# A diffusion-transformer layer on one core: twelve buffers for the modulation's weights, and another order of the MLP's buffers

## The chip, the cores and the metric

One Trainium2 chip, one of its cores. The metric is the device time of one execution in microseconds (us), as the median of several runs. The core's engines are PE (matrix multiply, with its weight loads shown as PEld), DVE, ACT and POOL (elementwise work), and SP, whose queue here issues most of the DMA transfers. Each engine takes its instructions strictly in order, and so does SP's queue.

## The reference, cut to what matters

One layer over 2048 latent tokens and 256 context tokens, 1024 channels, in float32. What the change and the prediction touch:

```python
mod = silu(c) @ w_mod + b_mod              # w_mod is 1024 x 6144
sh1, sc1, g1, sh2, sc2, g2 = split(mod, 6)
p = modulate(x, sh1, sc1) @ w_in           # layer norm, then scale and shift
y = concat(neighbourhood_attention(p), rwkv_mixer(p)) @ w_out
x = layer_norm(ALPHA * x + g1 * y)
h = squared_relu(modulate(x, sh2, sc2) @ mlp_w1)
x = layer_norm(ALPHA * x + g2 * (h @ mlp_w2))
```

`modulate` needs the first 2048 columns of `w_mod` (8 MB) before the first input projection can begin.

## The kernel before, in words

The work runs in five stages, one after the other on PE: modulation (to about 47 us), the input projection with the RWKV terms (`phase1`, to about 1003 us), attention together with the RWKV chain and the output projection (`tail`, to about 2110 us), the first MLP product (`mlp1`, to about 2771 us) and the second (`mlp2`, to the end).

**Who sets the order.** The program is traced in Python; a planner then fixes, before the run, the order of instructions on every engine and in SP's queue from its own estimate of when each is ready. Earlier lines of the program have the higher priority. Semaphore waits are added for data and for memory. On chip the order is fixed: an instruction whose wait is not over holds up all that stands behind it on its engine or queue.

**Memory.** SBUF pools are laid one behind the other from the left end of each partition, in the order in which they are opened (those with `side="right"` from the right end). When a pool is closed its bytes are free for the next one. With `reuse_waits="tile"` a tile waits for the last users of exactly those earlier tiles whose bytes it takes.

**Modulation** (lines 125 to 161). Sixteen loads of 512 KB of `w_mod` (line 146) go through SP; each feeds four PE instructions on `psd` (line 117). Their buffers are shared: eight of the loads alternate between the two `wst` buffers of pool `wp`, eight between one `th` and one `pa` buffer of pool `rk`, so four are in flight or in use at a time. While they come, PE also transposes the first six input tiles (`xturn`, line 386). When all is summed, the input is scaled and written as two parts, `xh` and `xl` (`ln1`, lines 417 to 421), tiles of 24.7 KB a partition each, which lie first in pool `k1`, at the left end. The input projection reads them (line 450) until its last matrix multiply.

**Start of `tail`.** Its left pools (`at1`: masks, queries `qz`, keys `kr`; `at2`: bias table `bu`, context keys `kc`) and its right pools (chain and accumulators) are laid over what `phase1` has left.

**`mlp1`** (line 1423) multiplies by a 7-product scheme (products 1, 5, 6, 3, 7, 2, 4, in that order) for each of 32 weight groups; a unit is one product of one group, 12 matrix multiplies. The groups 0 and 1 are begun together: units 0 to 2 are products 1, 5, 6 of group 0, units 3 to 5 the same of group 1, units 6 to 9 products 3, 7, 2, 4 of group 0, units 10 to 13 those of group 1. Each unit takes on DVE a sum or difference of weight blocks (`w1s`, lines 1448 to 1457), on ACT a rounded copy `w1h` and on DVE the rest `w1l` (line 1462), into ten `w1u` buffers of 2 KB. The weights of even groups lie in pool `xp` on the right, those of odd groups in `w1src` (`w1load`, line 1419; 1 MB each). The inputs of products 1, 5, 6 (`xh`, `xl` of each) are made ahead by `xstep`; those of products 3, 7, 2, 4 are read back from memory in four loads of 1 MB (line 1469), straight into `xl`, and then split on ACT and DVE (`xsplit`, lines 1475 and 1477). The last output tile is still being finished then: its rows `xres` are stored at line 1354, and later normalised as `xlast` (lines 1500 to 1504; POOL at line 1363, DVE at 1364, store at 1365) with rows `l1gb` loaded at line 1497.

Left to right, the pools of `mlp1` are before: `x2` (eight tiles of 8 KB: xh3, xl3, xh7, xl7, xh2, xl2, xh4, xl4), `w1src` (8 KB), `w1sum` (8 KB), `w1u` (20 KB), `h1`, `osm2`. Under them lay the output projection's pools: `yacc1` (16 KB), `woh` and `wol` (32 KB each), `l1g`, `l1b`, small ones, then the two `xres` buffers. So the last four `w1u` buffers lie on the `xres` buffers; the planner hands out `w1u` buffers 0, 9, 8, 7, 6 and so on downwards.

**`mlp2`** (line 1602) puts its results `acc` on the left end and behind them six buffers of 8 KB for its weights (`wp`, line 1625, 1 MB each), handed out 0, 5, 4, 3, 2, 1; its first input loads `al` (line 1597) come behind the weights in SP's queue. Weight buffer 0 lies on xh4, which the very last unit of `mlp1` reads.

Of the kernel before, what the change touches and what calls it, by code (L numbers as in the profile page):

```python
# [8 lines left out]
F32 = mybir.dt.float32  # L9
F32R = mybir.dt.float32r  # L10
# [5 lines left out]
D = 1024  # L16
# [5 lines left out]
W = 772  # L22
# [35 lines left out]
def f32(ap):  # L58
    return ap.bitcast(F32)


class Kern:
# [62 lines left out]
    def modulation(self, meanwhile):  # L125
        nc, a = self.nc, self.a
        t = self.sm.tile([128, 16], F32, name="silt")
        cc = self.vec[:, VOFF["c"]:VOFF["c"] + 16]
        nc.scalar.activation(t, cc, AF.Tanh, scale=0.5)
        nc.vector.tensor_scalar(t, t, 0.5, 0.5, ALU.mult, ALU.add)  # L130
        nc.vector.tensor_tensor(self.sil.rearrange("p k v -> p v k"), cc.rearrange("p (v k) -> p v k", v=2),
                                t.rearrange("p (v k) -> p v k", v=2), ALU.mult)
        acc = self.psD.tile([128, 512], F32, name="psd")
        nc.vector.memset(acc, 0.0)
        meanwhile()
        bm = self.r1.tile([128, 512], F32, tag="ei", name="bm")
        self.modbias(0, 2, bm)
        i = 0
        for k in range(8):
            for s in range(2):  # L140
                if i % 2 == 0:
                    w = self.wp.tile([128, D], F32, tag="wst", name="wmod")
                else:
                    w = self.rk.tile([128, 2, 768], F32R, tag=("th", "pa")[i // 2 % 2], name="wmod")
                    w = f32(w.rearrange("p a b -> p (a b)"))[:, :D]
                self.first = nc.sync.dma_start(w, a["w_mod"][k * 128:(k + 1) * 128, s * D:(s + 1) * D]).ins
                for j in range(2):
                    self.modacc(acc, k, s * 2 + j, w[:, j * 512:(j + 1) * 512], 2)
                i += 1
        nc.vector.tensor_tensor(bm, acc, bm, ALU.add)  # L150
        tp = self.psC.tile([128, 512], F32, name="psc")
        for b in range(4):
            nc.tensor.transpose(tp[:, b * 128:(b + 1) * 128], bm[:, b * 128:(b + 1) * 128], self.ident)

        tv = tp.rearrange("p (b j v) -> p j v b", b=4, j=4)
        for j in range(4):
            o = self.m1[:, j // 2 * 2:j // 2 * 2 + 2, j % 2 * 4:j % 2 * 4 + 4]
            if j < 2:
                nc.vector.tensor_copy(o, tv[:, j, 0:2, :])
            else:  # L160
                nc.vector.tensor_scalar(o, tv[:, j, 0:2, :], 1.0, None, ALU.add)
# [52 lines left out]
    def phase1(self):  # L214
        nc, tc, a = self.nc, self.tc, self.a
        with ExitStack() as es:
            P = lambda name, bufs, **kw: self.pool(es, name, bufs, **kw)
            k1 = P("k1", 1)
            self.xh = k1.tile([128, 8, W], F32R, name="xh")
            self.xl = k1.tile([128, 8, W], F32R, name="xl")  # L220
            self.halo = k1.tile([128, 8, 4], F32, name="halo")
            self.wp = P("wp", 2)
            self.xnp = P("xnp", 2)
            self.sm = P("sm", 4)
            self.rowp = P("rowp", 2)
            self.rk = P("rk", 1)
            self.r1 = P("r1", 1)
            self.sv = P("sv", 1)
            self.psM = P("psM", 2, space=PSUM)
            self.psB = P("psB", 3, space=PSUM)  # L230
            self.psC = P("psC", 2, space=PSUM)
            self.psD = P("psD", 1, space=PSUM)
            self.psS, self.psname = self.psB, "psb"
            ORD = (0, 2, 1)
            jobs = [(sb, b) for sb in ORD for b in self.blocks()]
            self.xs = {}
            self.wq = {}
            self.modulation(lambda: (self.wload(jobs[0], True), [self.xload(0, j) for j in range(6)], self.halo_rows(),
                                     self.xturn()))
            self.p1consts(k1)  # L240
            self.halo_cols()
            self.rq, self.sq, self.mq = [], [], []
            self.swait = 2
            self.lag = None
            for n, (sb, b) in enumerate(jobs):
                if b == jobs[0][1]:
                    self.ln1(sb)
                    nxt = ORD.index(sb) + 1
                    self.speed = (0, 1, SPEED)[nxt - 1]
                    if nxt > 1:  # L250
                        self.sq += [self.solve(*x) for x in SOLVES[nxt - 2]]
                if n == 4:
                    self.mq.append(self.modulation2())
                if b == XAT and nxt < 3:
                    self.mq.append(self.xloads(ORD[nxt]))
                if n + 1 < len(jobs):
                    self.wload(jobs[n + 1])
                for _ in self.job(sb, b):
                    self.side()
            while self.rq or self.mq or self.sq or self.lag:  # L260
                self.side()
# [1161 lines left out]
    def mlp1(self, es):  # L1423
        nc, a = self.nc, self.a
        V = nc.vector
        P = lambda name, **kw: self.pool(es, name, 1, **kw)
        x2 = P("x2")
        for pr in MORD[3:]:
            self.xu[pr] = [x2.tile([128, 4, 512], F32R, name="x%s%d" % (v, pr)) for v in "hl"]
        self.srcp, sp, up, zp = P("w1src"), P("w1sum"), P("w1u"), P("h1")  # L1430
        osm = self.pool(es, "osm2", 2)
        psP = P("psP", space=PSUM)
        self.psN = psP
# [34 lines left out]
        def xload(q, pr):  # L1468
            nc.sync.dma_start(f32(self.xu[pr][1]), self.XU[q][:, XU[pr]])
# [9 lines left out]
        def square(z):  # L1479
            V.scalar_tensor_tensor(z, z, 0.0, z, ALU.max, ALU.mult)  # L1480

        for pr in MORD[3:]:
            xload(0, pr)
        self.w1load(1)

        todo = {n + 2: [lambda pr=pr, n=n: xsplit(pr, n + 3)] for n, pr in enumerate(MORD[3:])}
        for n in range(M1LEAD):
# [2 lines left out]
        for n, (g, pr) in enumerate(seq):  # L1490
            prep(n + M1LEAD)
            q, fg = g // 16, g % 16
            if pr == 1:
# [20 lines left out]
                elif g == 20:  # L1514

                    w = self.base.tile([128, 2, 1024], F32, tag="uk", name="wp")
# [10 lines left out]
            xh, xl = self.xu[pr]  # L1527
            i = 0
# [405 lines left out]
```

## Time and profile before

| what | value |
|---|---|
| median of 3 runs | 3431.05 us (3422.89 to 3433.24) |
| profiled execution, its time | 3430.26 us |
| its span in the trace | 3428.5 us |
| mean granted PE clock | 0.963 |
| DVE, ACT busy | 76%, 44% |
| DMA, mean over the span | 164 GB/s |

The profile is one execution. A line of a timeline gives the start, the time it took, engine, line, operation, what it wrote and read, and in brackets how long the engine had been idle before it and what ended the wait. A busy PE is a pipelined one; the weight loads overlap it.

### The profile page before, as it was taken

The numbers are of one execution on the slowest core, as the hardware profiler recorded it, in microseconds if no ns is written. First come the engines' busy times: TensorE is split into PE (matmuls) and PEld (weight loads), VectorE is DVE, ScalarE is ACT, GpSimd is POOL, SyncE is SP. The second block draws the span as 40 slices with busy tenths as digits, with TensorE's granted clock in tenths as the row PEclk, the third lists the DMA queues.
The fourth block names the chain that finished last, engine by engine and source line by source line (L and its number), as shares of the span: only waits on it lengthen the run. The fifth ranks groups of instructions, "written<-read, shape, count | busy, mean of one in ns | idle before, by whom it ended". The sixth has DMA issues, their size and how long they took to land. (4 is left out here: it accounts for less than half of the span.)

```text
span 3428.5 us, 65249 instructions
## 1 busy us (share of the span) xinstructions
PE 3193.7 (93%) x25176; PEld 2605.3 (76%) x25176; DVE 2603.2 (76%) x4907; ACT 1523.1 (44%) x2891; POOL 511.6 (15%) x535
## 2 busy tenths in 40 slices
PE   7999899899978999989879988999999989999998
PEld 3888888789866777767657766777788868888886
DVE  5567977888687778767768877767767657899878
ACT  4555465456535445454442123343433343337333
POOL 0000000000005454544343322000000000010001
PEclk9999999999989999999989988999999999999999
DMA  7487376726666655554374546665644455545441
GB/s 242 134 246 209 95 178 161 223 76 168 169 191 156 140 133 129 138 131 117 98 202 147 172 155 217 213 205 186 215 155 137 154 193 162 167 153 210 148 155 73
DMA packets 765338, 561.67 MB, mean 164 GB/s; under 512 B 380412, under 2 KB 653564, under 8 KB 763620
## 3 DMA queue, kind: packets, MB, share of 16 engines
q1 hardware_dynamic: 691738, 523.14, 51.8%
q10 hardware_dynamic: 73290, 34.37, 3.5%
q8 instruction: 198, 3.24, 0.4%
q14 instruction: 112, 0.92, 0.1%
HBM read 359.70 MB, written 197.66 MB: 163 GB/s over the span
## 5 line engine op out<-in xcount | busy, mean ns | idle before, releaser
L450 PE MATMUL psm<-xh,wh 128*128 128x386 f32 (+1 forms) x1104 | 381.7, 348 | 16.5 <-ACT row L453 9.9
L450 PE MATMUL psm<-xl,wh 128*128 128x386 f32 (+1 forms) x1104 | 381.4, 346 | 2.7 <-DVE xl L421 2.6
L450 PE MATMUL psm<-xh,wl 128*128 128x386 f32 (+1 forms) x1104 | 377.0, 341 | 0.0
L450 PEld LDWEIGHTS psm<-xh,wh 128*128 128x128 f32 x1104 | 210.9, 192 | 42.7 <-ACT row L453 18.7
L450 PEld LDWEIGHTS psm<-xl,wh 128*128 128x128 f32 x1104 | 210.7, 191 | 17.8 <-issue 7.3
L450 PEld LDWEIGHTS psm<-xh,wl 128*128 128x128 f32 x1104 | 210.6, 191 | 4.9 <-issue 3.7
L1531 PE MATMUL psa<-xh,w1h 128*128 128x512 f32 x512 | 204.3, 399 | 4.0 <-DVE p L1557 3.7
L1795 POOL TENSOR_TENSOR acc<-acc,g 128x1024 f32<-128x1024 f32 x8 | 28.9, 3641 | 1186.9 <-DVE acc L1738 1186.9
L1531 PE MATMUL psa<-xl,w1h 128*128 128x512 f32 x512 | 202.7, 396 | 0.0
L1531 PE MATMUL psa<-xh,w1l 128*128 128x512 f32 x512 | 201.8, 395 | 0.0
L1679 ACT CAST ah<-al 128x1024 fp32r<-128x1024 f32 x98 | 103.0, 1051 | 216.5 <-DMA al<-HU 204.8
L760 DVE TENSOR_TENSOR stmp<-mp,xp 128x1 f32<-128x1 f32 (+30 forms) x310 | 179.2, 578 | 18.3 <-POOL xp L752 6.8
L1680 DVE TENSOR_TENSOR al<-al,ah 128x1024 fp32r<-128x1024 f32 x98 | 121.3, 1237 | 86.8 <-ACT ah L1679 86.7
L436 DVE TENSOR_TENSOR wl<-wst,wh 128x1024 fp32r<-128x1024 f32 x81 | 98.7, 1219 | 92.0 <-ACT wh L435 69.6
L1462 ACT CAST w1h<-w1s 128x512 fp32r<-128x512 f32 x96 | 59.6, 621 | 238.3 <-DVE w1s L1451 84.5
L1729 PE MATMUL psqb<-uh,ah 128*128 128x512 f32 x384 | 149.6, 392 | 9.1 <-ACT uh L1635 9.1
L1729 PE MATMUL psqa<-uh,ah 128*128 128x512 f32 x400 | 154.8, 391 | 3.2 <-ACT uh L1635 3.2
L1729 PE MATMUL psqa<-ul,ah 128*128 128x512 f32 x400 | 157.3, 393 | 0.3 <-DVE ul L1635 0.3
L1729 PE MATMUL psqa<-uh,al 128*128 128x512 f32 x400 | 157.0, 392 | 0.0
L761 DVE TENSOR_REDUCE xp<-stmp 128x1 f32<-128x1 f32 (+30 forms) x310 | 153.9, 496 | 3.3
L1729 PE MATMUL psqb<-ul,ah 128*128 128x512 f32 x384 | 150.5, 392 | 0.0
L1729 PE MATMUL psqb<-uh,al 128*128 128x512 f32 x384 | 150.3, 391 | 0.0
(393 smaller groups left out, 8818.4 us busy)
## 6 DMA issues: line engine op xcount, KB each, us to landing
al<-HU SPq DMA_DIRECT2D x106, 512.0 KB, 3.6
wst<-in_w_in SPq DMA_DIRECT2D x81, 512.0 KB, 4.3
w<-in_mlp_w SPq DMA_DIRECT2D x32, 1024.0 KB, 7.7
wp<-in_mlp_w SPq DMA_DIRECT2D x32, 1024.0 KB, 6.4
wmod<-in_w_mod SPq DMA_DIRECT2D x48, 512.0 KB, 5.3
HU<-p SPq DMA_DIRECT2D x96, 256.0 KB, 3.9
HU<-s SPq DMA_DIRECT2D x84, 256.0 KB, 2.0
bkc<-BK SPq DMA_DIRECT2D x36, 512.0 KB, 4.8
```

What stands on the lines that cost most here:

```text
L436: nc.vector.tensor_tensor(wl, w, f32(wh), ALU.subtract)
L450: nc.tensor.matmul(ps[:, :y - x], lhsT=s[:, k, :], rhs=m[:, k, x:y], start=(i == 0), stop=(i == 23))
L760: nc.vector.tensor_tensor(tv, mp[:, i:i + 1, lo:lo + n].to_broadcast([128, n, n]), xp[:, lo:lo + n, lo:lo + n], ALU.mult)
L761: nc.vector.tensor_reduce(xp[:, lo:lo + n, i], tv, AX.X, ALU.add)
L1462: made[n] = nc.scalar.copy(h, x).ins, V.tensor_tensor(l, x, f32(h), ALU.subtract).ins
L1531: nc.tensor.matmul(ps, lhsT=w[:, k, :], rhs=x[:, k, :], start=(i == 0 and pr in (1, 5, 2)), stop=(i == 11), skip_group_check=True)
L1679: fs += [lambda: nc.scalar.copy(ah, f32(al)), fb[0], lambda: V.tensor_tensor(al, f32(al), f32(ah), ALU.subtract), fb[1]]
L1680: lambda: V.tensor_tensor(al, f32(al), f32(ah), ALU.subtract), fb[1]]
L1729: nc.tensor.matmul(ps, lhsT=x[:, c, s], rhs=y[:, c, :], start=(i == 0 and new), stop=(i == 5 and end), skip_group_check=True)
L1795: (V if 4 * i + j in VMUL else G).tensor_tensor(row, row, g2, ALU.mult)
```

## The change

In `modulation` the sixteen loads get buffers of their own, twelve tiles of 4 KB in a new pool `modp`. That pool is opened last in `phase1`, closed after the modulation, and a pool `kx` with `xh` and `xl` is opened in its place; they no longer lie first in `k1`, and all other pools of `phase1` move 49,408 bytes to the left. In `mlp1` the pools are opened as `w1u`, `w1src`, `w1sum`, `x2`, `h1`, and the load of the second weight group stands ahead of the four input loads in the program.

```diff
-                if i % 2 == 0:
-                    w = self.wp.tile([128, D], F32, tag="wst", name="wmod")
-                else:
-                    w = self.rk.tile([128, 2, 768], F32R, tag=("th", "pa")[i // 2 % 2], name="wmod")
-                    w = f32(w.rearrange("p a b -> p (a b)"))[:, :D]
+                w = self.modp.tile([128, D], F32, name="wmod")
                 self.first = nc.sync.dma_start(w, a["w_mod"][k * 128:(k + 1) * 128, s * D:(s + 1) * D]).ins
...
             k1 = P("k1", 1)
-            self.xh = k1.tile([128, 8, W], F32R, name="xh")
-            self.xl = k1.tile([128, 8, W], F32R, name="xl")
             self.halo = k1.tile([128, 8, 4], F32, name="halo")
...
-            self.modulation(lambda: (self.wload(jobs[0], True), [self.xload(0, j) for j in range(6)], self.halo_rows(),
-                                     self.xturn()))
+
+            with ExitStack() as em:
+                self.modp = self.pool(em, "modp", 12)
+                self.modulation(lambda: (self.wload(jobs[0], True), [self.xload(0, j) for j in range(6)], self.halo_rows(),
+                                         self.xturn()))
+            kx = P("kx", 1)
+            self.xh = kx.tile([128, 8, W], F32R, name="xh")
+            self.xl = kx.tile([128, 8, W], F32R, name="xl")
             self.p1consts(k1)
...
-        x2 = P("x2")
+        up, self.srcp, sp, x2, zp = P("w1u"), P("w1src"), P("w1sum"), P("x2"), P("h1")
         for pr in MORD[3:]:
             self.xu[pr] = [x2.tile([128, 4, 512], F32R, name="x%s%d" % (v, pr)) for v in "hl"]
-        self.srcp, sp, up, zp = P("w1src"), P("w1sum"), P("w1u"), P("h1")
...
+        self.w1load(1)
         for pr in MORD[3:]:
             xload(0, pr)
-        self.w1load(1)
```

## Rows read from the trace of the kernel before

**Rows 1.** The page's busy time by engine, over the whole span.

```profile
PE 3193.7 (93%) x25176; PEld 2605.3 (76%) x25176; DVE 2603.2 (76%) x4907; ACT 1523.1 (44%) x2891; POOL 511.6 (15%) x535
```

**Rows 2.** Busy time in windows: PE, PEld, DVE, ACT, POOL, clock, DMA share, GB/s.

```profile
25.50:44.60 19.10, 15.05 (x75) 4.36 (x73) 0.00 (x0) 5.98 (x13) 0.00 (x0) 0.94 0.87 279
21.00:25.50 4.50, 3.07 (x18) 1.21 (x15) 1.23 (x2) 1.30 (x3) 0.42 (x1) 1.00 0.96 354
```

**Rows 3.** Timeline of SP's queue, the first 75 us.

```profile
9.84 3.34 SPq L146 DMA_DIRECT2D wmod<-in_w_mod  x4
...
17.42 20.05 SPq L146 DMA_DIRECT2D wmod<-in_w_mod  x12
```

**Rows 4.** Waits of SP's queue, 0 to 60 us: total, times, longest.

```profile
SPq L146 <- PE psd L117: 10.9, 8, 3.4
```

**Rows 5.** Timeline of PE, 14 to 75 us.

```profile
15.51 1.88 PE L117 MATMUL psd<-wmod,sil 128*2 128x512 f32 x4 [15.51 <-DMA wmod<-in_w_mod]
...
44.65 1.87 PE L117 MATMUL psd<-wmod,sil 128*2 128x512 f32 x4 [0.78 <-DMA wmod<-in_w_mod]
...
50.94 1.08 PE L450 MATMUL psm<-xh,wh 128*128 128x386 f32 x2 [1.50 <-DVE xh L420]
```

**Rows 6.** Timeline of PE, 985 to 1035 us.

```profile
1017.19 0.58 PE L986 MATMUL psl<-kr,qz 128*128 128x256 f32 x1 [14.46 <-ACT qz L960]
```

**Rows 7.** Timeline of SP's queue, 975 to 1040 us.

```profile
1007.22 0.43 SPq L937 DMA_DIRECT2D bu<-in_rpb  x1
...
1009.43 5.85 SPq L958 DMA_DIRECT2D qz<-Q  x6
```

**Rows 8.** Waits of PE, 2105 to 2800 us: total, times, longest.

```profile
PE psb L1531 <- ACT w1h L1462: 12.9, 1, 12.9
PE psqb L1729 <- ACT uh L1635: 9.1, 1, 9.1
PE pse L1531 <- ACT w1h L1462: 5.4, 2, 5.2
```

**Rows 9.** Timeline of ACT, 2103 to 2176 us.

```profile
2123.03 0.62 ACT L1462 CAST w1h<-w1s 128x512 fp32r<-128x512 f32 x1 [13.03 <-DMA X<-xres]
```

**Rows 10.** Timeline of SP's queue, 2103 to 2160 us.

```profile
2111.24 0.50 SPq L1419 DMA_DIRECT2D w<-in_mlp_w  x1
2114.58 0.33 SPq L1469 DMA_DIRECT2D xl<-XU  x1
2115.01 0.38 SPq L1354 DMA_DIRECT2D X<-xres  x1
2115.44 2.03 SPq L1469 DMA_DIRECT2D xl<-XU  x3
...
2137.95 0.33 SPq L1365 DMA_DIRECT2D X<-xlast  x1
```

**Rows 11.** Line 1469, the loads of the inputs' parts, whole span.

```profile
DMA to landing us min/median/max: 8.2/10.0/11.9
```

**Rows 12.** Timeline of DVE, 2103 to 2176 us.

```profile
2111.60 0.68 DVE L1448 TENSOR_TENSOR w1s<-w 128x512 f32<-128x512 f32 x1
2118.86 0.69 DVE L1448 TENSOR_TENSOR w1s<-w 128x512 f32<-128x512 f32 x1 [6.58 <-DMA w<-in_mlp_w]
...
2123.68 0.69 DVE L1462 TENSOR_TENSOR w1l<-w1s,w1h 128x512 fp32r<-128x512 f32 x1 [2.34 <-ACT w1h L1462]
...
2143.16 2.23 DVE L1477 TENSOR_TENSOR xl<-xl,xh 128x2048 fp32r<-128x2048 f32 x1
```

**Rows 13.** Busy time in windows at the start of the first MLP product.

```profile
2119.00:2124.00 5.00, 0.30 (x1) 0.30 (x2) 2.66 (x5) 0.62 (x1) 0.00 (x0) 0.50 1.01 421
2124.00:2164.00 40.00, 40.00 (x165) 32.10 (x165) 37.99 (x53) 20.24 (x29) 3.85 (x1) 0.95 0.58 211
```

**Rows 14.** Timeline of PE, 2752 to 2802 us.

```profile
2768.43 0.50 PE L1531 MATMUL psa<-xh,w1h 128*128 128x512 f32 x1 [0.79 <-DVE p L1557]
```

**Rows 15.** The chain that ended last, 2755 to 2800 us: start, us, what.

```profile
2771.52 0.38 SPq L1625
...
2782.08 13.15 DMA al<-HU
```

## The prediction

> **What bounds the kernel now.** I read the page's busy time first: PE is busy for 93% of the span, DVE for 76% [rows 1]. Work that PE does anyway isn't touched by this change, so what it can win lies in the remaining 7%. I therefore looked next for PE's waits, stage by stage, and they lie at the joints: PE waits 15.5 us for its first weights [rows 5], 14.46 us at the start of attention [rows 6], 12.9 and 5.4 us at the start of the first MLP product and 9.1 us at the start of the second [rows 8]. The change touches buffers at each of these joints, so each is a term of its own. The sum is made against the profiled execution, 3430.26 us (1.8 us more than its span); the median of the runs shown is 0.8 us above it. About 0.3%, 10.3 us, is what a measurement of this kernel can tell from no change.
>
> **Term 1, modulation.** Four buffers serve sixteen loads. SP issues four at once, then needs 20.05 us for the other twelve [rows 3], because it waits eight times, 10.9 us in all, for PE to finish with a buffer [rows 4]. In 25.50 to 44.60 the core moves only 279 GB/s [rows 2], so 19.10 x 279 = 5.33 MB. Twelve buffers take away all but the last four of these waits, and those buffers were used by the first four loads, long done. So the loads queue back to back, and bytes set the time. In the 4.5 us before, where all four buffers were being filled, the rate was 354 GB/s [rows 2]; the highest that I saw with loads of this size queued was 421 GB/s [rows 13]. At 354 the same bytes take 15.1 us (gain 4.0), at 421 they take 12.7 us (gain 6.4). PE has its own limit: of the 19.10 us it is busy for 15.05 [rows 2], its share of transposes included, so 4.05 us can be closed there and about 1.4 us of gaps before. I take 4.5, between 4.0 and 6.4 and nearer to the rate of the same loads. Below, the bound is 0: the transposes wait on ACT in PE's order, and if they set the pace the loads are hidden. Behind the last weight group (44.65 to 46.52) comes the same chain as before: bias, transposes, first scaled input, first projection at 50.94 [rows 5]. It moves as a block. New there: xh and xl now lie on the weight buffers, so anything that writes them must wait for the last modulation matrix multiply; the scaling needs that result anyway, so this costs 0.
>
> Here a page bears on how row and rate are to be read: the DMA share in this stretch is 0.87 [rows 2]. Taken as a bound it would leave 0.13 x 19.10 = 2.5 us to win and put the total 2 us later. The Trainium skill, page "Perfetto Trace Analysis", section "Identifying the Most-Contended Engine", says that with sixteen DMA engines occupancy misleads and that bytes are the measure.
>
> Without that sentence the row of 354 GB/s at a share of 0.96 says the same: per unit of share 0.87 gave 321, 0.96 gave 369, 1.01 gave 417 [rows 2, 13], so a busy engine is not one at its rate.
>
> **Term 2, start of attention.** The pools of the first stage lie 49 KB further left, so the masks no longer lie on the inputs that the last projection reads. But bias table and queries were issued at 1007.22 and 1009.43 with SP hardly idle (six query loads take it 5.85 us) [rows 7], and the keys still lie under the last weights. Only the mask issues, some 0.8 us of SP, can move ahead. I take 0.5 us of the 14.46; ends: 2 us gained (two loads' issue), 1 us lost (one issue behind a wait that is new).
>
> **Term 3, start of the first MLP product.** ACT stands for 13.03 us before it may write a w1u buffer, because that buffer lies on xres, whose store has to land first [rows 9]. The store is issued at 2115.01, behind a load of 1 MB [rows 10]; loads of that size land in 8.2 to 11.9 us [rows 11]. After the change no w1u buffer lies there, and ACT's wait and PE's 12.9 us [rows 8] lose their cause. What is late next is DVE. It is busy for 37.99 of the 40 us that follow [rows 13], so the stage can only be moved ahead by the DVE idle time that gets filled. That is 2.34 us before 2123.68, which waits for ACT's late copy, whole; and of the 6.58 us before 2118.86, spent on the second group's weights, what DVE can do meanwhile: the low parts (w1l) of group 0, which are held back by ACT only [rows 12]. At least four operations of 0.6 to 0.7 us are 2.4 us, at most the whole 6.58. So 4.7 to 8.9; I take 6, nearer to the lower end since the sums of group 1 still need its weights.
>
> The Trainium skill, page "Perfetto Trace Analysis", section "Identifying the Most-Contended Engine", also says that a busy PE is no measure of its limit, and that weight-load time is. By PE's busy time the stretch from 2124 is full (40.00 of 40), and the whole wait of 12.9 us would be won; by the rule PE has room there (weight loads 32.10) [rows 13] and the wait is won only as far as another engine allows.
>
> The DVE row by itself gives that limit, and the sum goes by it.
>
> The second weight group stands ahead of the inputs in the program. But before, too, SP issued it at 2111.24, ahead of all four input loads [rows 10], and its buffer comes free when the output projection's weights do, as before: 0 (bounds: one input load's issue, 0.4 us, either way). What gains a wait is the fourth input load: its buffer xl4 now lies on xres. Behind it in SP's queue stand the norm's rows; it may issue only when the store has landed, about 2123, and then lands by 2135 [rows 10, 11]. DVE split it at 2143.16 [rows 12], which 6 us earlier is 2137. So it is hidden, by 2 us; without that cover it costs one for one. The granted clock of 0.50 in the gap before [rows 13] costs little: a mean of 0.95 over the next 40 us is 4 us at 1.2 GHz, 2 us of PE work in a stretch that DVE limits: 0, at most 2 gained.
>
> **Term 4, start of the second MLP product.** The first weight buffer waited for the last unit's end, issue 2771.52 [rows 15]. It now lies on inputs of the unit before, which is done some 0.8 us before the last unit starts at 2768.43 [rows 14], so 1 MB can leave 3.8 us earlier. The chain ends with the input load al, 13.15 us from its issue at 2782.08 to landing [rows 15], behind weights in the same DMA engines; PE waits 9.1 us for it [rows 8]. 1 MB less ahead of it is 2.5 us at 421 GB/s [rows 13]; two other weight buffers still wait for the last unit, so I take 2 (ends 0 and 3.8).
>
> **Sum.** 4.5 + 0.5 + 6 + 2 = 13; 3430.26 - 13 = 3417.3, and 0.8 to the median: 3418.
>
> **Rivals.**
> A, forecast: terms about as sized, 7 to 20 us, 3411 to 3424. Chance 0.56.
> B, all idle closes: 6.4 + 2 + 8.9 + 3.8 = 21, so 3410. For it: four separate causes are taken away. Against it: DVE has only 2 us of slack in 40 [rows 13]. Chance 0.12.
> C, the start of the first MLP product gives its gain back: DVE and ACT take their work in a fixed order, and if an operation on the second group's weights, or a split, stands before the low parts, the 6.58 us [rows 12] stay. Then 4.5 + 0.5 + 2 = 7, so 3424. Against it: ACT's cause is gone in any order. Chance 0.20.
> D, slower: the fourth input load is placed in SP's queue behind the store of the normalised rows, issued at 2137.95 [rows 10]. It lands after 8.2 to 11.9 us [rows 11], between 2146 and 2150, its low part is ready at about 2154 in place of 2145.4 [rows 12], and product 4 of group 0 holds up DVE and PE: 9 us against 7 from the other terms, some 3433. It decides from a landing later than 2141 (split due at 2143.16 less ACT's half), and each us past that is a us; with the splits of both groups held up it passes 3441. Against it: input loads stand earlier in the program. Chance 0.08.
> E, the change doesn't do what it says in the modulation: transposes or the DMA engines already set the pace and terms 1 and 2 are 0 to 2.5. Then 8 to 10.5 from the rest, 3421 to 3423. Against it: 10.9 us of SP's waits name PE as the cause [rows 4]. Chance 0.04.
>
> **How the numbers follow.** The time is A's, 3418. The range runs from 3406, B with the clock's 2 us and the scatter of the runs, to 3430, over C and E up to a half-lost D; outside lie D's slow end and a mishap not seen, 2 in 10. Faster by over 0.3% means under 3420.8: most of A (0.47) and B (0.12), with a little of E, 0.60. Slower, over 3441.3: the far end of D, 0.06. The rest, 0.34, is within 0.3%: C, E, the upper part of A and the near end of D.
>
> **What would show it.** Term 1: SP's sixteen loads with no wait on psd, and the first projection near 46.5 in place of 50.94. Term 2: the first attention product still waits about 14 us. Term 3: ACT's wait for the store of xres gone, PE's 12.9 us down to a few, DVE idle in the first 12 us of the stage under 5 us; wrong if DVE's 6.58 us stand. D is seen if the load of xl4 comes behind the store of xlast. Term 4: the first weight load before the last unit starts, and PE's 9.1 us down to about 7. Wrong altogether if PE's waits at these four joints sum to what they did, or if a new one stands at the products 2 or 4 of group 0.

## The result, and the profile after

The changed kernel takes 3413.38 us (median of 6 runs, 3404.98 to 3415.6) against 3430.53 us (median of 6) for the kernel before: 17.15 us less, a ratio of 0.9946 with a 95% interval of 0.9933 to 0.9959. The forecast was 3418 us and the range 3406 to 3430. The profiled execution of after took 3414.7 us, with a span of 3412.9.

PE's share is what the busy line shows first, as [rows 1]; its work is the same, so the idle part shrank.

```profile
PE 3192.8 (94%) x25176; PEld 2602.5 (76%) x25176; DVE 2599.1 (76%) x4907; ACT 1523.7 (45%) x2891; POOL 511.0 (15%) x535
```

To see where the time went I cut both spans at four events of PE: the first matrix multiply of the input projection, of attention, of the first and of the second MLP product. Each number is a difference of two starts in PE's timeline (before: 50.94, 1017.19, 2110.06, 2774.72; after: 48.07, 1011.73, 2100.27, 2758.06).

| stage, us | before | after | difference |
|---|---|---|---|
| modulation | 50.9 | 48.1 | -2.9 |
| phase1 | 966.3 | 963.7 | -2.6 |
| attention and output projection | 1092.9 | 1088.5 | -4.3 |
| first MLP product | 664.7 | 657.8 | -6.9 |
| second MLP product | 653.8 | 654.8 | +1.0 |

Together they are the 15.6 us between the two spans.

**Modulation.** SP's queue in the changed kernel (as [rows 3]):

```profile
9.95 9.93 SPq L142 DMA_DIRECT2D wmod<-in_w_mod  x12
20.83 5.26 SPq L432 DMA_DIRECT2D wst<-in_w_in  x2
26.21 4.88 SPq L751 DMA_DIRECT2D XB<-xp  x2
31.19 2.76 SPq L142 DMA_DIRECT2D wmod<-in_w_mod  x4
```

Twelve loads go out in one row and the wait of 10.9 us for PE [rows 4] is gone. But ahead of the last four now stand two loads of projection weights (`wst`, whose buffers are no longer lent to the modulation) and two small stores. The same windows as [rows 2]:

```profile
21.00:25.50 4.50, 4.50 (x28) 1.46 (x28) 1.60 (x4) 1.45 (x3) 0.00 (x0) 1.00 1.02 409
25.50:44.60 19.10, 14.70 (x82) 5.20 (x80) 2.65 (x7) 6.30 (x13) 0.52 (x7) 1.00 1.03 331
```

331 GB/s in place of 279, at a granted clock of 1.00. PE's timeline has the last modulation multiplies and the start of the projection in place of [rows 5], at once at 0.34 us a multiply where it was 0.53 (at 52.55 us), and the start of attention in place of [rows 6], whose wait has not moved:

```profile
41.78 1.03 PE L117 MATMUL psd<-wmod,sil 128*2 128x512 f32 x4 [0.22 <-DMA wmod<-in_w_mod]
...
47.11 1.03 PE L117 MATMUL psd<-wmod,sil 128*1 128x512 f32 x4 [1.25 <-DMA wmod<-in_w_mod]
48.07 0.62 PE L450 MATMUL psm<-xh,wh 128*128 128x386 f32 x2
48.53 0.34 PE L450 MATMUL psm<-xl,wh 128*128 128x386 f32 x1
...
1011.73 0.58 PE L986 MATMUL psl<-kr,qz 128*128 128x256 f32 x1 [14.85 <-ACT qz L960]
```

The last modulation multiplies end 3.7 us earlier (42.81 in place of 46.52), the projection starts only 2.9 us earlier: in PE's order two sets of four multiplies of the second modulation (the `128*1` of line 117, a side job of `phase1`) now stand ahead of it, and for the weights of the second set PE waits 1.25 us.

**The MLP's joints.** PE's waits there (as [rows 8]; 2080 to 2180, then 2690 to 2800 us):

```profile
PE psb L1530 <- DVE xl L1476: 3.5, 1, 3.5
PE psa L1530 <- DVE w1l L1461: 2.5, 1, 2.5
...
PE psqb L1728 <- ACT uh L1634: 7.5, 1, 7.5
```

The waits of 12.9 and 5.4 us on ACT's copies have gone, and what is late next is DVE, by 3.5 and 2.5 us. DVE's timeline (as [rows 12]) and POOL's:

```profile
2109.42 0.69 DVE L1447 TENSOR_TENSOR w1s<-w 128x512 f32<-128x512 f32 x1 [3.67 <-DMA w<-in_mlp_w]
...
2118.53 4.24 DVE L1476 TENSOR_TENSOR xl<-xl,xh 128x2048 fp32r<-128x2048 f32 x1
...
2124.43 2.28 DVE L1476 TENSOR_TENSOR xl<-xl,xh 128x2048 fp32r<-128x2048 f32 x1
```

```profile
2117.91 2.71 POOL L1363 TENSOR_TENSOR xlast<-xlast,l1gb 128x1024 f32<-128x1024 f32 x1 [28.84 <-DVE xlast L1362]
```

The first split of an input took 4.24 us where the next took 2.28, and that split is the one PE waited 3.5 us for. It ran beside a multiply on POOL. SP's queue at both joints (as [rows 10, 15]):

```profile
2105.79 0.38 SPq L1354 DMA_DIRECT2D X<-xres  x1
2106.22 0.49 SPq L1496 DMA_DIRECT2D l1gb<-in_ln_b  x1
2106.77 5.67 SPq L1468 DMA_DIRECT2D xl<-XU  x4
...
2753.21 2.55 SPq L1624 DMA_DIRECT2D wp<-in_mlp_w  x3
...
2764.33 34.39 SPq L1596 DMA_DIRECT2D al<-HU  x9
```

### The profile page after: what moved, and what is told of

It reads as the page before. It is cut to its first block, busy times and chain, and to the rows that moved or that the text cites. A ratio compares the mean times of both kernels' runs of the same rounds, so it can differ in the third digit from the quotient of the medians.

```text
span 3412.9 us, 65231 instructions
## 1 busy us (share of the span) xinstructions
PE 3192.8 (94%) x25176; PEld 2602.5 (76%) x25176; DVE 2599.1 (76%) x4907; ACT 1523.7 (45%) x2891; POOL 511.0 (15%) x535
## 4 chain that ended last, share of the span: by engine, by line
PE 65%; DVE 14%; DMA 11%; SPq 3%; issue 3%; ACT 2%; POOL 1%; ACTq 0%; DVEq 0%; POOLq 0%
PE psm L450 14%; PE psa L1530 8%; PE psqb L1728 7%; PE psqa L1728 7%; PE psb L1530 4%; PE ops L1346 4%; PE pse L1530 2%; PE psv L1051 2%; DMA ks<-AR 1%; PE psm L468 1%; DMA w<-in_mlp_w 1%; PE pst L1022 1%; PE psg L1141 1%; PE psl L986 1%; PE psd L117 1%
```

## The experiments

The same cut for every kernel that ran. Ratios are to the kernel before, measured beside each run. A stage is read from one execution, so two questions were open from the start: how far a stage scatters when nothing in it changes, and whether the 6.9 us of phase1 and attention, which no term of the forecast held, belong to the change.

| run | to first projection | phase1 + attention | first MLP product | second | ratio, 95% interval |
|---|---|---|---|---|---|
| before | 50.9 | 2059.1 | 664.7 | 653.8 | |
| after | 48.1 | 2052.2 | 657.8 | 654.8 | 0.9946 (0.9933 to 0.9959) |
| e1 modulation only | 46.9 | 2046.9 | 664.4 | 654.8 | 0.9965 (0.9953 to 0.9977) |
| e2 MLP only | 49.5 | 2067.7 | 654.9 | 654.9 | 0.9962 (0.9948 to 0.9977) |
| e3 four buffers | 51.1 | 2066.4 | 654.8 | 653.4 | 1.0002 (0.9991 to 1.0014) |
| e4 x4 first | 46.4 | 2047.1 | 655.6 | 656.7 | 0.9945 (0.9932 to 0.9959) |
| e5 multiply on DVE | 45.2 | 2044.2 | 652.6 | 654.2 | 0.9942 (0.9925 to 0.9960) |
| e6 x4 under acc | 48.9 | 2048.2 | 663.8 | 648.2 | 0.9950 (0.9938 to 0.9962) |
| e7 weights unbroken | 41.6 | 2083.4 | 655.4 | 654.5 | 1.0020 (1.0009 to 1.0030) |
| e8 eight buffers | 47.4 | 2077.2 | 652.6 | 655.2 | 1.0001 (0.9988 to 1.0013) |
| e9 ten buffers | 46.2 | 2058.5 | 655.3 | 655.7 | 0.9965 (0.9952 to 0.9978) |
| e10 order, one job later | 46.1 | 2102.8 | 654.2 | 654.4 | 1.0051 (1.0036 to 1.0066) |
| e11 order, one job earlier | 48.7 | 2057.1 | 654.7 | 653.9 | 0.9953 (0.9938 to 0.9967) |
| e12 before, other order | 49.1 | 2081.3 | 664.6 | 654.0 | 1.0065 (1.0046 to 1.0084) |

e9 to e12 ran on another chip, where the kernel before took 3440.05 us (15 runs), 0.28% more; their long stages compare with the others only to about 6 us.

**The two parts alone.** e1 takes the old four lines of pools and loads in the MLP, e2 the old modulation.

```diff
-        up, self.srcp, sp, x2, zp = P("w1u"), P("w1src"), P("w1sum"), P("x2"), P("h1")
+        x2 = P("x2")
         for pr in MORD[3:]:
             self.xu[pr] = [x2.tile([128, 4, 512], F32R, name="x%s%d" % (v, pr)) for v in "hl"]
+        self.srcp, sp, up, zp = P("w1src"), P("w1sum"), P("w1u"), P("h1")
```

> Only the modulation part: twelve buffers in a pool of their own, the inputs' parts in their place; the MLP as before. Theory 1 (the parts add, and what phase1 and attention gained beyond the forecast, 2.6 and 4.3 us, belongs to the moved pools of this part): first projection near 48.1 us, first attention product near 1011.7, first MLP unit near 2100.3, PE's wait of 12.9 us on the MLP's first copies back, time 3430.5 - 9.8 = 3420.7 us. Theory 2 (those 6.9 us are scatter between executions, or belong to the MLP part): first projection near 48.1, the stages after it as long as before, time 3427.6 us.

> Only the MLP part: pools in the order w1u, w1src, w1sum, x2, h1 and the second weight group ahead of the input loads; modulation as before. Theory 1 (the parts add): first projection at 50.9 us, first attention product near 1017, first MLP unit near 2110, then the first MLP product 6.8 us shorter, time near 3424 us. Theory 2 (the attention stage gained because of the MLP's buffers): first MLP unit near 2106, time near 3419.5 us. If term 3 was wrong and the modulation did it all: no change, 3430 us.

e1 took 3419.35 us and e2 3416.01, against 3429.78 for the kernel before. In e1 the MLP's waits on ACT are back:

```profile
PE psb L1531 <- ACT w1h L1462: 13.1, 1, 13.1
PE pse L1531 <- ACT w1h L1462: 4.9, 1, 4.9
```

The parts work each in its own stage: the projection starts 3 to 4 us earlier in e1 alone, the first MLP product is 9.8 us shorter in e2 alone. In e1, phase1 and attention gained 12 us, so Theory 1 of that run fits its total of -10 us. The medians don't simply add: -10.4 and -13.8 us apart, -17.15 together, though the intervals leave room for it. e2's time is below what either of its theories asked for (3424 and 3419.5). And e2 warns of such readings: up to the first MLP product it has the kernel before's instructions in the kernel before's order, and still its attention stage took 1105.6 us where the other execution took 1092.9. The windows over that stage, before and then e2 (us, busy time of PE, PEld, DVE, ACT, POOL, granted clock, DMA share, GB/s):

```profile
1017.19:2110.06 1092.87, 987.62 (x12665) 762.71 (x12665) 833.51 (x2100) 451.87 (x1175) 464.41 (x488) 0.94 0.55 146
```

```profile
1011.64:2117.19 1105.55, 1002.24 (x12665) 773.14 (x12665) 831.41 (x2100) 451.67 (x1175) 464.02 (x488) 0.92 0.55 144
```

The same 12665 multiplies kept PE busy 14.6 us longer at a granted clock of 0.92 in place of 0.94. That execution took 3428.75 us, the longest of e2's 11, 12.7 above their median. Twelve us of scatter in one execution is more than any term of the forecast; the medians carry the verdict, the stages only say where to look.

**The number of buffers.** e3 has 4, e8 has 8 and e9 has 10 in place of 12.

```diff
-                self.modp = self.pool(em, "modp", 12)
+                self.modp = self.pool(em, "modp", 4)
```

> The changed kernel with four modulation buffers in place of twelve, at the same place. Theory 1 (the number of buffers is what counts): SP waits for PE between the loads again, first projection near 50.9 us, all else as in the changed kernel, time 3413.4 + 2.9 = 3416.3 us. Theory 2 (what counts is that the weights' pool no longer shares buffers with the first projection weights, so those loads go early): first projection near 48.1 us, 3413.4 us. Theory 3 (the gain in phase1 and attention comes from the place of the pools and not from the buffers): both keep their 6.9 us.

> The changed kernel with eight modulation buffers in place of twelve. Theory 1 (what counts is that PE isn't waited for): eight are enough, first projection at 46.4 to 48.1 us. Theory 2 (each buffer counts): half way, near 49 us. For the attention stage, which the four-buffer kernel ran in 1102 us: Theory A (its length goes with the planner's order, which differs again): anything between 1086 and 1106, without relation to the buffers, time 3408 to 3430 us. Theory B (it goes with the end of the modulation): between 1088 and 1102, time near 3420 us.

> The changed kernel with ten modulation buffers. Its order of instructions after the modulation is that of the changed kernel (on PE 37 lines of a comparison differ, on SP 19, all of them before or just after the modulation), where eight buffers gave another order (11170 lines on PE). Theory A (phase1 and attention go with the planner's order): phase1 and attention together 2044 to 2053 us as in the five executions of the changed order, against 2077 with eight buffers; time 3408 to 3416 us. Theory B (they go with the number of buffers): between the two, near 2063 us, time 3420 to 3425 us.

For the modulation the answer is plain: with four buffers, in either place, the projection starts at 49.1 to 51.1 us (before, e2, e3, e12), with eight or more at 45.2 to 48.9 (nine executions, e7 aside). For the total it is not: e3 gave back all 17 us, three of them in the modulation and 14 in phase1 and attention, and e8, whose modulation is as early as with twelve, gave back as much. None of the theories of e3 had that. Four and eight buffers give the planner other times of readiness and it wrote another order for what follows. Ten buffers keep the order of twelve and, at 0.9965, keep a gain of 15 us that eight lose (intervals apart). Its stages sum to 2058.5 us, outside the 2044 to 2053 that Theory A asked for, by about what the slower chip adds (2058.5 x 3430.5 / 3440.05 = 2052.8); so this run favours the order, and doesn't alone settle it.

**The order itself.** e10 and e11 change nothing of the modulation's loads and nothing of the MLP; the second modulation, a side job of phase1, starts one projection later or earlier. e12 does the first to the kernel before.

```diff
-                if n == 4:
+                if n == 5:
                     self.mq.append(self.modulation2())
```

> The changed kernel with the second modulation (the gates and the MLP's part) begun one projection later: work, buffers and first projection as before, but another order from there on (10963 lines on PE). Theory A (phase1 and attention go with the planner's order, whatever the change): first projection at 45 to 49 us, phase1 and attention together outside 2044 to 2053 us, by 5 us or more to either side; time outside 3408 to 3416 us. Theory B (the gain there is the change's own): 2044 to 2053 us, 3408 to 3416 us.

> The same with the second modulation begun one projection earlier (6153 lines differ on PE). Theory A: phase1 and attention together outside 2044 to 2053 us or at another place than in the run before, time outside 3408 to 3416 us. Theory B: 2044 to 2053 us, 3408 to 3416 us.

> The kernel before, without any of the change, with the second modulation begun one projection later (8825 lines differ on PE from the kernel before). Theory A (order): phase1 and attention together may leave the 2059 to 2068 us of the two executions of the kernel before's order by 5 us or more, time then outside 3425 to 3435 us. Theory B (the change's own gain): 2059 to 2068 us, time 3425 to 3435 us. First projection near 50 us and first MLP product near 664.5 us by both.

e10 took 3456.23 us: by the ratios 36 us over the changed kernel (0.0105 x 3430), and 31 us over e9, which keeps the changed kernel's order and ran beside it. Its only long stages are phase1 and attention. e12 took 3460.65, 21 us slower than its own baseline. e11 kept the changed kernel's time, so that run by itself fits its Theory B: another order need not cost anything. But the order that the planner happens to write can decide more than the change does, and Theory B of e10 falls. The windows over the attention stage, after and then e10:

```profile
1011.73:2100.27 1088.54, 983.50 (x12665) 760.22 (x12665) 827.87 (x2102) 453.65 (x1176) 463.06 (x484) 0.94 0.55 146
```

```profile
1027.56:2148.86 1121.30, 1005.88 (x12664) 774.26 (x12665) 837.13 (x2098) 455.06 (x1175) 467.10 (x484) 0.92 0.54 141
```

PE worked 22.4 us longer on the same multiplies at the lower clock, and was idle 115.4 us in place of 105.0. Largest in e10's waits and then in after's:

```profile
PE psg L1141 <- DMA ks<-AR: 32.3, 21, 6.2
PE psl L986 <- ACT qz L960: 20.1, 1, 20.1
```

```profile
PE psg L1141 <- DMA ks<-AR: 21.9, 19, 6.4
PE psl L986 <- ACT qz L960: 14.9, 1, 14.9
```

The other long attention stages are not all of one kind. In e3, e7 and e8 the extra time is nearly all PE's busy time, at a granted clock of 0.93 (998.4, 1005.2 and 995.9 us busy, 103.8, 107.7 and 107.7 idle); in e12 it is mostly idle time (990.8 busy, 123.7 idle). Whether an order brings its clock with it isn't shown: e2's execution had 0.92 in the kernel before's order. What rule would give a good order was not tried.

**The loads in one row.** e7 puts the `wst` loads, all but the first, and the `XB` stores behind the sixteenth modulation load (an order constraint on both, such as the kernel has on other loads).

```diff
-        nc.sync.dma_start(w, a["w_in"].rearrange("(k p) c -> p k c", p=128)[:, :, c0:c0 + 128])
+        d = lambda: nc.sync.dma_start(w, a["w_in"].rearrange("(k p) c -> p k c", p=128)[:, :, c0:c0 + 128])
+        if first:
+            d()
+        else:
+            with self.tc.issue_after(self.first):
+                d()
...
-            nc.sync.dma_start(self.XB[r:r + 32, d, q0:q0 + 32, ha * 32:ha * 32 + 32], xp[h * 32:h * 32 + 32])
+            with self.tc.issue_after(self.first):
+                nc.sync.dma_start(self.XB[r:r + 32, d, q0:q0 + 32, ha * 32:ha * 32 + 32], xp[h * 32:h * 32 + 32])
```

> The changed kernel with all sixteen modulation loads issued in one row, ahead of the two loads of projection weights (wst) and the two small stores (XB) that stood before the last four. Theory 1 (term 1 fell short because those took DMA time and SP's queue from the last four loads): last modulation matrix multiply some 2.5 us earlier, first projection at 44 to 45.5 us, the loads of wst then late for the second projection, time 3411 to 3413 us. Theory 2 (PE's transposes set the pace from 20 us on): first projection at 46.4 to 48.1 as in the changed kernel. Either way the planner's order of the attention stage changes; if that order alone moves its time, the stage (1087 to 1089 us in three executions of the changed order) moves by 5 us or more in either direction.

```profile
9.37 15.42 SPq L142 DMA_DIRECT2D wmod<-in_w_mod  x16
```

```profile
34.65 0.66 PE L386 MATMUL psc<-ident,xn 128*128 128x128 f32 x4
35.23 1.90 PE L117 MATMUL psd<-wmod,sil 128*2 128x512 f32 x16
...
41.61 0.98 PE L455 MATMUL psm<-xh,wh 128*128 128x386 f32 x2 [2.35 <-DVE xl L357]
```

The projection starts at 41.6 us, 2.4 us earlier than the earliest that Theory 1 asked for, so the two loads and two stores are what kept term 1 small, and the transposes were no limit in the changed kernel. In e7 they are: PE has no idle time from 15.01 to 37.13 us, and its last sixteen modulation multiplies go in one block behind the last transposes. The loads and the stores are not told apart. At 409 GB/s the 1 MB of the two loads is 2.6 us, and the last modulation multiply ends 5.7 us earlier in e7 than in the changed kernel (37.13 in place of 42.81), so the bytes of the loads alone don't make it up. The total is worse all the same, 3435.58 us: phase1 and attention took 2083 us in the order that came with it.

**The multiply beside the split.**

```diff
-        nc.gpsimd.tensor_tensor(xt, xt, g, ALU.mult)
+        (eng or nc.gpsimd).tensor_tensor(xt, xt, g, ALU.mult)
...
-                    self.norm1(x, slice(r, r + 128), xn, rows[:, 0], rows[:, 1], osm)
+                    self.norm1(x, slice(r, r + 128), xn, rows[:, 0], rows[:, 1], osm, V)
```

> The changed kernel with one multiply of the last rows' norm (xlast by l1gb) on DVE in place of POOL, both times; all before the MLP is the same program. In the changed kernel the first split of an input's low part took DVE 4.24 us in place of 2.28, while POOL ran that multiply, and PE waited 3.5 us for it. Theory 1 (the two engines hold each other up when they work at once): all four splits take 2.28 us, the multiply costs DVE 1.2 us, PE's wait of 3.5 us falls to 1.5 to 2.8, first MLP product 0.7 to 2 us shorter, time near 3412 us. Theory 2 (the split was long for another reason, such as the input loads that land beside it): the first split stays at 4.2 us and the stage gets 1.2 us longer, 3414.6 us.

DVE's timeline and PE's wait in e5:

```profile
2107.47 1.22 DVE L1363 TENSOR_TENSOR xlast<-xlast,l1gb 128x1024 f32<-128x1024 f32 x1
2108.61 2.28 DVE L1476 TENSOR_TENSOR xl<-xl,xh 128x2048 fp32r<-128x2048 f32 x1
```

```profile
PE psb L1530 <- DVE xl L1476: 1.7, 1, 1.7
```

Theory 1 holds: the multiply costs DVE 1.22 us, the split is back at 2.28, PE's wait falls from 3.5 to 1.7 us, and the stage took 652.6 us (e8 had that without it, so its length proves nothing by itself). The median, 3408.89 us, agrees with the changed kernel's within the intervals; no run was faster than the changed kernel by more than the measurement tells.

**The joint to the second product.** e4 has the inputs' tiles in another order, so that the first weight buffer waits for the last unit; e6 gives product 4's inputs a pool of their own ahead of `w1src`, so that none of the six does.

```diff
-        for pr in MORD[3:]:
+        for pr in (4, 3, 7, 2):
             self.xu[pr] = [x2.tile([128, 4, 512], F32R, name="x%s%d" % (v, pr)) for v in "hl"]
```

> The changed kernel with the four inputs' tiles in the order 4, 3, 7, 2, so that the first weight buffer of the second MLP product lies on inputs of product 4, which the last unit reads. Undoes term 4 alone. Theory 1 (the early first load is what cut PE's wait from 9.1 to 7.5 us): the first weight load goes only after the last unit's end, PE's wait is 9.1 us again, time 3413.4 + 1.6 = 3415.0 us. Theory 2 (the wait is set by something else, such as the place of the stores in SP's queue): the wait stays at 7.5 us and the time at 3413.4 us.

> The changed kernel with product 4's inputs in a pool of their own behind w1u, so that they lie under the second product's results and none of its six weight buffers lies on what the last unit reads. Theory 1 (the weight loads at the joint to the second product wait for the last unit): all six weight loads are issued before the last unit ends, some 1.6 us earlier as a block, PE's wait of 7.5 us falls to about 6, time near 3412 us. Theory 2 (the stores ahead of them in SP's queue set their start): first weight load again about 1.6 us ahead of the last unit's end and nothing more, 3413.4 us. Theory 3 (another place of the inputs costs at the stage's start what it gives at its end): the input loads come later, and PE waits for a split of product 2.

PE's waits in e4, then in e9, whose MLP is the changed kernel's, then in e6:

```profile
PE psqb L1728 <- ACT uh L1634: 9.1, 1, 9.1
```

```profile
PE psqb L1728 <- ACT uh L1634: 9.6, 1, 9.6
```

```profile
PE psqa L1728 <- ACT uh L1634: 11.1, 1, 11.1
PE psqb L1728 <- ACT uh L1634: 2.1, 1, 2.1
```

In e4 the first load leaves at the last unit's end again and the wait is 9.1 us, as Theory 1 said, but that shows nothing: the other executions with the new pools, whose first load leaves 0.5 to 1.9 us ahead of that end, wait 9.2 (e2), 8.8 (e3), 8.4 (e5), 8.6 (e7), 9.3 (e8), 9.6 (e9), 8.8 (e10) and 8.8 us (e11), and those with the old pools 9.1 (before), 9.0 (e1) and 8.1 (e12). The 7.5 us of the changed kernel is scatter of one execution. The time of e4, 3408.06 us, is no longer than the changed kernel's. In e6 all six weight loads are issued ahead of the last unit's end, as Theory 1 asked, and PE waits 13.2 us in all against 10.7 in the changed kernel (3.2 and 7.5). Both MLP products together take 1312.0 us there and 1312.6 in the changed kernel. An expectation missed: loads that leave earlier at this joint bring no time in any run here.

The load of the second weight group was not tried apart from the pools.

## Why the prediction was right

**Term 1 (4.5): 3.1.** The mean start is 50.2 us with four buffers (50.9, 49.5, 51.1, 49.1) and 47.1 with twelve or ten (48.1, 46.9, 46.4, 45.2, 48.9, 46.2, 46.1, 48.7). The mechanism was right. The step that was mis-sized is "so the loads queue back to back": I looked only at who waits for the sixteen loads' buffers, and not at who else had waited for them. The freed `wst` buffers let 1 MB of other loads in ahead of the last four, and two stores stood there too; e7 shows what they cost together. "It moves as a block" failed by 0.8 us, for the multiplies of the second modulation that came in between. The 421 GB/s of [rows 13] were misread: those are loads of 1 MB and not "of this size"; loads of 512 KB ran at 409 after the change. PE's 15.05 us of work in the stretch was no bound: by it 4.05 + 1.4 us could be won, and in e7 the last modulation multiply ends 9.4 us earlier (37.13 in place of 46.52). Sixteen of these multiplies take 1.90 us in one block, and four by themselves 1.03. By the DMA share of 0.87 no more than 2.5 us were to be had here; with the loads in one row e7 had 8.6 (50.2 to 41.6), so the share was no bound. On this the trace agrees with what the Trainium skill, page "Perfetto Trace Analysis", section "Identifying the Most-Contended Engine", says of occupancy and bytes; the 3.1 us of the changed kernel alone would not have told the two apart.

**Term 2 (0.5): none.** The wait is 14.85 us in place of 14.46. What did change here, phase1 and attention, was not in the sum at all.

**Term 3 (6): 9.5.** The first MLP product takes 664.6 us without the new pools (before, e1, e12) and 655.0 with them (mean of after, e2 to e4 and e7 to e11; e5 and e6 change the stage or its end). ACT's wait went and DVE is what is late next, as forecast; the fourth input load waited for the store and was hidden, so rival D fell. The step that failed is the size, "the stage can only be moved ahead by the DVE idle time that gets filled", which stopped at 2164: PE's second wait, 5.2 of the 5.4 us of [rows 8], lies behind it, at 2175. It stands with the old pools (4.9 us in e1, 5.7 in e12) and is gone in all runs with the new ones but e6 (2.7). That it came from the same lag is argued, not shown. After the change DVE is still idle for 3.67 us before the second weight group lands, so of the 8.9 us at most 5.3 were filled (2.34 and 2.91 of the 6.58), and the idle time filled is not the whole gain.

**Term 4 (2): none seen.** The second product takes 654.2 us without (before, e1, e12) and 654.6 with the change (mean of after, e2, e3 and e7 to e11). The first load left 1.6 us ahead of the last unit's end and not 3.8, since SP stood at the stores ahead of it. The step that failed is "1 MB less ahead of it is 2.5 us": PE's wait doesn't follow the first load's issue: beside the 7.5 us of the changed kernel it is 8.4 to 9.6 us in the eight others where that load leaves early, and 8.1 to 9.1 us in the four where it doesn't. The sign "PE's 9.1 us down to about 7" came with 7.5 in the changed kernel's execution by luck.

**The sum.** 3.1 + 9.5 - 0.4 = 12, near the 13 of the forecast. The other 5 of the 17 us (the ratio's interval is 14 to 23 us), and in e1 some 9 of its 12 (by its ratio), lie by subtraction in phase1 and attention, where the forecast had 0.5. That the order there changes was foreseen by no term; it could as well have been 20 us the other way, as e3, e7, e8 and e10 show. So the total came out in the range partly by luck: the rival that was missing is "the planner writes another order", on either side.

## What to carry to other kernels

Where a planner orders the whole program, compare the order of the stages that a change doesn't touch before crediting it with their time, and repeat the measurement with a change that only disturbs the order: here that alone was worth 31 to 36 us beside 12 us of gain from the parts themselves. A buffer that is no longer shared frees its other user too; look at which transfers were held back by the sharing, because they come in next. Where a wait is taken from one engine, follow the next late engine past the first full window, and the waits behind it.

## What was not expected of the hardware

A DVE operation on two tensors and one on POOL hold each other up. The split takes 2.28 us alone; begun at 2118.53, while POOL's multiply ran until 2120.62, it took 4.24 us, that is to 2.15 us after POOL's end. The same pair made it 4.3 to 4.5 us in e2, e4 and e6, and taking POOL's part away made it 2.28 (e5). In e8 it went the other way: the split kept its 2.28 us and POOL's multiply took 5.53 in place of 2.71.

```profile
2142.23 2.28 DVE L1476 TENSOR_TENSOR xl<-xl,xh 128x2048 fp32r<-128x2048 f32 x1
```

```profile
2141.84 5.53 POOL L1363 TENSOR_TENSOR xlast<-xlast,l1gb 128x1024 f32<-128x1024 f32 x1 [33.35 <-DVE xlast L1362]
```

The Trainium skill, page "SBUF — State Buffer", section "Who interferes with whom", says that a DVE instruction with two inputs in SBUF contends with a POOL instruction that reads SBUF, and that the order of issue decides which of the two is held up. The traces agree that either can be the one; the starts in a timeline don't tell which, since in e8 POOL's is shown 0.39 us ahead, about as in e4 (0.38), where DVE was held.

The granted clock of PE in the attention stage moved between 0.92 and 0.94 from one execution to the next of the same instructions, and 0.02 of it was 14.6 us of PE's busy time.
